# Loading x in 64 KB runs and y through one buffer, in a kernel for the softmax of row-wise dot products

## The chip, the cores and the metric

The kernel runs on one core of a Trainium2 chip. The metric is the device time of one execution in microseconds (us), and the median of several executions is quoted. The profile of an execution has a span, from the first instruction to the last, that is shorter than its time, because the time also holds what lies before and after these.

A load is issued into a queue, and 16 DMA engines work the queue off in packets, each of which the trace records. The load has landed when its semaphore, a counter that others wait on, has been raised. For each load an engine also moves a 4-byte completion packet, which takes 9 ns.

## The reference

```python
B, N, D = 8, 4096, 512            # x and y: [8, 4096, 512], float32
gram = np.matmul(x, y.transpose(0, 2, 1))
diag = np.diagonal(gram, axis1=1, axis2=2)
diag = diag - diag.max(axis=-1, keepdims=True)
exp = np.exp(diag)
return exp / exp.sum(axis=-1, keepdims=True)     # [8, 4096]
```

Only the diagonal is needed: 4096 dot products of length 512 per batch, then a softmax over the 4096. So 134.2 MB are read, each byte is used once, and 0.13 MB are written.

## The kernel before

A batch is laid out with 32 rows on each of 128 partitions, and the 32 rows of a partition are one contiguous run of 64 KB in memory. The kernel takes half a batch at a time, so x and y each come in 4 MB loads made of 128 runs of 32 KB. Three pairs of buffers rotate.

```python
R = N // P          # 32 rows per partition
H = R // 2          # half a batch: 16 rows
io = tile_pool(bufs=3)

def load(b, r0, parts):
    xt = io.tile([P, H, D], f32);  yt = io.tile([P, H, D], f32)
    o = 0
    for n in parts:
        nc.sync.dma_start(out=xt[:, o:o+n, :], in_=xv[b, :, r0+o : r0+o+n, :])
        nc.sync.dma_start(out=yt[:, o:o+n, :], in_=yv[b, :, r0+o : r0+o+n, :])
        o += n
    return xt, yt

def dots(b, r0, xt, yt):                 # the wide form: product in place, then the sum
    nc.vector.tensor_tensor(out=xt, in0=xt, in1=yt, op=mult)
    nc.vector.tensor_reduce(out=diag[:, c:c+H], in_=xt, axis=X, op=add)

# dots_by_row: one scalar_tensor_tensor per row, with accum_out (product and sum at once)
# softmax(b): max on VectorE, all-reduce on GpSimd, -max on VectorE, exp with sum on ScalarE,
#             all-reduce on GpSimd, reciprocal and scaling on VectorE, store from ScalarE's queue
# ... (cut)
for b in range(B):
    for h in range(2):
        n = 2 * b + h
        parts = {2*B-2: [8, 8], 2*B-1: [8, 4, 2, 1, 1]}.get(n, [H])
        xt, yt = load(b, h * H, parts)
        (dots_by_row if n >= 2*B-3 else dots)(b, h * H, xt, yt)
    softmax(b)
```

Of the kernel before, what the change touches and what calls it, by code (L numbers as in the profile page):

```python
# [1 line left out]

# [5 lines left out]


@with_exitstack
def kernel(
    ctx: ExitStack,
    tc: tile.TileContext,
    x: bass.AP,
    y: bass.AP,
    out: bass.AP,
):
    nc = tc.nc
    f32 = mybir.dt.float32  # L20
    B, N, D = x.shape
    P = nc.NUM_PARTITIONS
    R = N // P
    H = R // 2


    xv = x.rearrange("b (p r) d -> b p r d", p=P)
    yv = y.rearrange("b (p r) d -> b p r d", p=P)
    ov = out.rearrange("b (p r) -> b p r", p=P)

    io = ctx.enter_context(tc.tile_pool(name="io", bufs=3))
    persist = ctx.enter_context(tc.tile_pool(name="persist", bufs=1))
    sm = ctx.enter_context(tc.tile_pool(name="sm", bufs=2))

    diag = persist.tile([P, B * R], f32, name="diag")
    res = persist.tile([P, B * R], f32, name="res")

    def load(b, r0, parts):
        xt = io.tile([P, H, D], f32, tag="xt", name="xt")
        yt = io.tile([P, H, D], f32, tag="yt", name="yt")  # L40
        o = 0
        for n in parts:
            nc.sync.dma_start(out=xt[:, o : o + n, :], in_=xv[b, :, r0 + o : r0 + o + n, :])  # L43
            nc.sync.dma_start(out=yt[:, o : o + n, :], in_=yv[b, :, r0 + o : r0 + o + n, :])  # L44
            o += n
        return xt, yt

    def dots(b, r0, xt, yt):
        c = b * R + r0
        nc.vector.tensor_tensor(out=xt, in0=xt, in1=yt, op=mybir.AluOpType.mult)  # L50
        nc.vector.tensor_reduce(  # L51
            out=diag[:, c : c + H], in_=xt, axis=mybir.AxisListType.X, op=mybir.AluOpType.add
        )

    def dots_by_row(b, r0, xt, yt):
        for k in range(H):
            c = b * R + r0 + k
            nc.vector.scalar_tensor_tensor(  # L58
                out=xt[:, k, :],
                in0=xt[:, k, :],  # L60
                scalar=1.0,
                in1=yt[:, k, :],
                op0=mybir.AluOpType.mult,
                op1=mybir.AluOpType.mult,
                accum_out=diag[:, c : c + 1],
            )

    def softmax(b):
        db = diag[:, b * R : (b + 1) * R]
        rb = res[:, b * R : (b + 1) * R]  # L70
        mxp = sm.tile([P, 1], f32, tag="mxp", name="mxp")
        nc.vector.tensor_reduce(out=mxp, in_=db, axis=mybir.AxisListType.X, op=mybir.AluOpType.max)  # L72
        mx = sm.tile([P, 1], f32, tag="mx", name="mx")
        nc.gpsimd.partition_all_reduce(out_ap=mx, in_ap=mxp, channels=P, reduce_op=bass_isa.ReduceOp.max)  # L74
        nmx = sm.tile([P, 1], f32, tag="nmx", name="nmx")
        nc.vector.tensor_single_scalar(out=nmx, in_=mx, scalar=-1.0, op=mybir.AluOpType.mult)  # L76
        sump = sm.tile([P, 1], f32, tag="sump", name="sump")
        nc.scalar.activation(  # L78
            out=rb, in_=db, func=mybir.ActivationFunctionType.Exp,
            bias=nmx, scale=1.0, accum_out=sump,  # L80
        )
        ssum = sm.tile([P, 1], f32, tag="ssum", name="ssum")
        nc.gpsimd.partition_all_reduce(out_ap=ssum, in_ap=sump, channels=P, reduce_op=bass_isa.ReduceOp.add)  # L83
        rc = sm.tile([P, 1], f32, tag="rc", name="rc")
        nc.vector.reciprocal(out=rc, in_=ssum)  # L85
        nc.vector.tensor_single_scalar(out=rb, in_=rb, scalar=rc, op=mybir.AluOpType.mult)  # L86
        nc.scalar.dma_start(out=ov[b], in_=rb)

    for b in range(B):
        for h in range(2):  # L90
            n = 2 * b + h
            parts = {2 * B - 2: [8, 8], 2 * B - 1: [8, 4, 2, 1, 1]}.get(n, [H])
            xt, yt = load(b, h * H, parts)
            (dots_by_row if n >= 2 * B - 3 else dots)(b, h * H, xt, yt)
        softmax(b)


# [1 line left out]
_INS = ['x', 'y']  # L99
_OUTS = [((8, 4096), 'float32')]  # L100


# [23 lines left out]
```

## Time and profile before

| | |
|---|---|
| time | 323.26 us, median of 3 runs (323.23 to 323.59) |
| span of the profile | 321.6 us (an execution of 323.94 us) |
| load queue busy | 97.5% of the 16 DMA engines' span |
| VectorE busy | 261.4 us (81%) |

These lines are from the page of the kernel before: the span, the busy times, the rates in 40 slices of the span, and the table of DMA queues (queue, packets, MB, share of 16 engines' span). q1 carries the loads, q10 the stores.

```profile
span 321.6 us, 345 instructions
DVE 261.4 (81%) x154; ACT 4.6 (1%) x17; POOL 6.1 (2%) x20
...
DMA  8999999999999999999999999999999999999991
GB/s 326 456 395 452 440 408 456 391 458 391 456 412 436 454 395 456 440 408 458 416 432 456 392 458 440 408 456 417 433 449 395 456 437 412 424 424 426 427 407 53
...
q1 hardware_dynamic: 6048, 134.22, 97.5%
q10 hardware_dynamic: 1152, 0.13, 0.3%
```

The load queue is busy from the start to the end. The packets of q1 add up to 313.5 us per engine. VectorE (DVE) has work for 261 us only.

The list of waits (engine, line, what was waited for: us in total, times, longest) shows VectorE waiting for y, and its groups of instructions show what it does. Each group has the line, the operation, the operands and the count, then the busy time in us and the mean of one in ns, then the idle time before them.

```profile
DVE xt L50 <- DMA yt<-in_y_dram: 34.5, 8, 22.6
DVE xt L58 <- DMA yt<-in_y_dram: 9.7, 4, 4.7
```

```profile
L50 DVE TENSOR_TENSOR xt<-xt,yt 128x8192 f32<-128x8192 f32 x13 | 113.0, 8689 | 34.5 <-DMA yt<-in_y_dram 34.5
L51 DVE TENSOR_REDUCE diag<-xt 128x16 f32<-128x8192 f32 x13 | 112.9, 8686 | 0.4
L58 DVE SCALAR_TENSOR_TENSOR xt<-xt,yt 128x512 f32<-128x512 f32 x48 | 30.0, 687 | 9.9 <-DMA yt<-in_y_dram 9.7
```

The chain that ended last, in order of time (start in us, duration, what), contains the wide products and sums:

```profile
42.03 8.70 DVE xt L50
50.74 0.02 issue
50.76 8.70 DVE diag L51
...
79.12 0.33 SPq L43
79.44 0.05 issue
79.50 40.70 DMA yt<-in_y_dram
```

This chain says that a sum on VectorE releases a buffer and that a load is then issued. The load takes 40.7 us from issue to landing, but 4 MB take only 9.7 us at the rate of this trace. For the rest of the time the load stands in the queue behind others.

The packet records give the cost of a run (here a contiguous stretch of memory). A packet of 32 KB takes 1213 ns (median), 16 KB 612, 8 KB 312, 4 KB 161 and 2 KB 86.

### The profile page before, as it was taken

The numbers are of one execution on the slowest core, as the hardware profiler recorded it, in microseconds if no ns is written. First come the engines' busy times: TensorE is split into PE (matmuls) and PEld (weight loads), VectorE is DVE, ScalarE is ACT, GpSimd is POOL, SyncE is SP. The second block draws the span as 40 slices with busy tenths as digits, with TensorE's granted clock in tenths as the row PEclk, the third lists the DMA queues.
The fourth block names the chain that finished last, engine by engine and source line by source line (L and its number), as shares of the span: only waits on it lengthen the run. The fifth ranks groups of instructions, "written<-read, shape, count | busy, mean of one in ns | idle before, by whom it ended". The sixth has DMA issues, their size and how long they took to land.

```text
span 321.6 us, 345 instructions
## 1 busy us (share of the span) xinstructions
DVE 261.4 (81%) x154; ACT 4.6 (1%) x17; POOL 6.1 (2%) x20
## 2 busy tenths in 40 slices
DVE  0019979898998979979799897989979799776494
ACT  1000000000000000000000000000000000000000
POOL 0000000000000000000000000000000000000000
DMA  8999999999999999999999999999999999999991
GB/s 326 456 395 452 440 408 456 391 458 391 456 412 436 454 395 456 440 408 458 416 432 456 392 458 440 408 456 417 433 449 395 456 437 412 424 424 426 427 407 53
DMA packets 7201, 134.36 MB, mean 418 GB/s; under 512 B 1824, under 2 KB 1824, under 8 KB 2592
## 3 DMA queue, kind: packets, MB, share of 16 engines
q1 hardware_dynamic: 6048, 134.22, 97.5%
q10 hardware_dynamic: 1152, 0.13, 0.3%
q14 instruction: 1, 0.01, 0.0%
HBM read 134.22 MB, written 0.13 MB: 418 GB/s over the span
## 4 chain that ended last, share of the span: by engine, by line
DMA 63%; DVE 33%; issue 1%; SPq 1%; POOL 1%; ACT 0%; POOLq 0%; DVEq 0%
DMA yt<-in_y_dram 63%; DVE xt L50 16%; DVE diag L51 16%; SPq L43 1%; POOL mx L74 0%; POOL ssum L83 0%; DVE mxp L72 0%; DVE xt L58 0%; ACT res L78 0%; DVE rc L85 0%; POOLq L121 0%; SPq L44 0%; DVE res L86 0%; DVE nmx L76 0%; DVEq L50 0%
## 5 line engine op out<-in xcount | busy, mean ns | idle before, releaser
L50 DVE TENSOR_TENSOR xt<-xt,yt 128x8192 f32<-128x8192 f32 x13 | 113.0, 8689 | 34.5 <-DMA yt<-in_y_dram 34.5
L51 DVE TENSOR_REDUCE diag<-xt 128x16 f32<-128x8192 f32 x13 | 112.9, 8686 | 0.4
L58 DVE SCALAR_TENSOR_TENSOR xt<-xt,yt 128x512 f32<-128x512 f32 x48 | 30.0, 687 | 9.9 <-DMA yt<-in_y_dram 9.7
L74 POOL PARTITION_ALL_REDUCE mx<-mxp x8 | 2.8, 352 | 306.6 <-DVE mxp L72 306.6
L85 DVE RECIPROCAL rc<-ssum 128x1 f32<-128x1 f32 x8 | 1.3, 164 | 7.7 <-POOL ssum L83 7.7
L78 ACT ACTIVATE res<-diag,nmx 128x32 f32<-128x32 f32 x8 | 2.6, 321 | 312.9 <-DVE nmx L76 312.9
L76 DVE TENSOR_SCALAR nmx<-mx 128x1 f32<-128x1 f32 x8 | 1.2, 154 | 4.3 <-POOL mx L74 4.3
L58 DVE DVE_READ_ACCUMULATOR xt<-xt,yt 128x1 f32 x48 | 3.9, 82 | 0.0
L83 POOL PARTITION_ALL_REDUCE ssum<-sump x8 | 3.1, 385 | 5.8 <-ACT res L78 5.8
L86 DVE TENSOR_SCALAR res<-res,rc 128x32 f32<-128x32 f32 x8 | 1.9, 242 | 0.9
L72 DVE TENSOR_REDUCE mxp<-diag 128x1 f32<-128x32 f32 x8 | 1.5, 186 | 0.3
L78 ACT ACTIVATION_READ_ACCUMULATOR res<-diag,nmx 128x1 f32 x8 | 1.5, 186 | 0.0
L78 ACT ACT_TABLE_LOAD x1 | 1.3, 1283 | 0.7 <-PEq L110 0.7
L110 POOL MEMSET const-float32-0.0<- 128x1 f32 x1 | 0.1, 100 | 0.2 <-issue 0.2
L110 POOL MEMSET const-bfloat16-1.0<- 128x1 bf16 x1 | 0.1, 102 | 0.0
L110 POOL MEMSET const-uint8-127<- 128x1 uint8 x1 | 0.1, 102 | 0.0
L110 POOL MEMSET const-float32-1.0<- 128x1 f32 x1 | 0.1, 99 | 0.0
## 6 DMA issues: line engine op xcount, KB each, us to landing
xt<-in_x_dram SPq DMA_DIRECT2D x14, 4096.0 KB, 31.2
yt<-in_y_dram SPq DMA_DIRECT2D x14, 4096.0 KB, 40.5
xt<-in_x_dram SPq DMA_DIRECT2D x3, 2048.0 KB, 27.1
yt<-in_y_dram SPq DMA_DIRECT2D x3, 2048.0 KB, 31.6
xt<-in_x_dram SPq DMA_DIRECT2D x1, 1024.0 KB, 31.9
yt<-in_y_dram SPq DMA_DIRECT2D x1, 1024.0 KB, 29.5
xt<-in_x_dram SPq DMA_DIRECT2D x1, 512.0 KB, 25.8
yt<-in_y_dram SPq DMA_DIRECT2D x1, 512.0 KB, 22.2
```

Of the source, the lines that this page charges most:

```text
L43: nc.sync.dma_start(out=xt[:, o : o + n, :], in_=xv[b, :, r0 + o : r0 + o + n, :])
L50: nc.vector.tensor_tensor(out=xt, in0=xt, in1=yt, op=mybir.AluOpType.mult)
L51: nc.vector.tensor_reduce(out=diag[:, c : c + H], in_=xt, axis=mybir.AxisListType.X, op=mybir.AluOpType.add)
L58: nc.vector.scalar_tensor_tensor(out=xt[:, k, :], in0=xt[:, k, :], scalar=1.0, in1=yt[:, k, :], op0=mybir.AluOpType.mult, op1=mybir.AluOpT ...
L72: nc.vector.tensor_reduce(out=mxp, in_=db, axis=mybir.AxisListType.X, op=mybir.AluOpType.max)
L74: nc.gpsimd.partition_all_reduce(out_ap=mx, in_ap=mxp, channels=P, reduce_op=bass_isa.ReduceOp.max)
L76: nc.vector.tensor_single_scalar(out=nmx, in_=mx, scalar=-1.0, op=mybir.AluOpType.mult)
L78: nc.scalar.activation(out=rb, in_=db, func=mybir.ActivationFunctionType.Exp, bias=nmx, scale=1.0, accum_out=sump,)
L83: nc.gpsimd.partition_all_reduce(out_ap=ssum, in_ap=sump, channels=P, reduce_op=bass_isa.ReduceOp.add)
L85: nc.vector.reciprocal(out=rc, in_=ssum)
L86: nc.vector.tensor_single_scalar(out=rb, in_=rb, scalar=rc, op=mybir.AluOpType.mult)
L110: nc = _bacc.Bacc("TRN2", target_bir_lowering=False, num_devices=1)
```

## The change

The intent is fewer and longer packets, and a softmax that disturbs VectorE less often. x of a batch is loaded at once, in runs of 64 KB, into one of two 64 KB buffers per partition. y has only one 64 KB buffer, which is filled in halves. Together they take the 192 KB per partition that the six buffers took before. Products are written over x. The softmaxes of batches 0 to 4 and of 5 and 6 are done in two groups with one store each, and the order on each engine is fixed by hand. All of batch 6 is done row by row.

```diff
-    xt = io.tile([P, H, D]);  yt = io.tile([P, H, D])         # three of each
+    xs = [big.tile([P, R, D], f32, name=f"xs{i}") for i in range(2)]
+    ys = big.tile([P, R, D], f32, name="ys")
 ... (cut)
-    for b in range(B):
-        for h in range(2):
-            ... load(b, h * H, parts); dots or dots_by_row
-        softmax(b)
+    for b in range(wide):                       # wide = B - 2
+        load_x(b, 0, R)                         # 8 MB in 64 KB runs
+        for r0 in (0, R // 2):
+            load_y(b, r0, R // 2)               # 4 MB in 32 KB runs
+            dots_wide(b, r0, R // 2)            # products over x
+        if b == wide - 1:
+            group_out("a", 0, wide - 1, first)  # scale and store batches 0 to 4
+        sums_wide(b)                            # one sum for the whole batch
+        if b == wide - 2:
+            first = group_exp("a", 0, wide - 1)
+    b = B - 2
+    load_x(b, 0, R)
+    ... load_y in halves, dot_row for each of the 32 rows
+    b = B - 1
+    r0 = 0
+    for n in (8, 8, 8, 4, 2, 1, 1):
+        load_x(b, r0, n);  load_y(b, r0, n)
+        for r in range(r0, r0 + n):
+            if r == 2:
+                second = group_exp("b", B - 3, 2)
+            if r == 10:
+                group_out("b", B - 3, 2, second)
+            dot_row(b, r)
+        r0 += n
+    last_softmax(b)
```

In the groups, ScalarE does the negation and the scaling, which VectorE did before.

More of the change, by code (lines that the diff above doesn't have):

```diff
@@ L19 @@
     nc = tc.nc
+    ctx.enter_context(tc.manual_schedule())
     f32 = mybir.dt.float32
+    Alu = mybir.AluOpType
+    Act = mybir.ActivationFunctionType
+    X = mybir.AxisListType.X
     B, N, D = x.shape
@@ L23 @@
     R = N // P
-    H = R // 2
+    wide = B - 2
     xv = x.rearrange("b (p r) d -> b p r d", p=P)
     yv = y.rearrange("b (p r) d -> b p r d", p=P)
-    ov = out.rearrange("b (p r) -> b p r", p=P)
-    io = ctx.enter_context(tc.tile_pool(name="io", bufs=3))
-    persist = ctx.enter_context(tc.tile_pool(name="persist", bufs=1))
-    sm = ctx.enter_context(tc.tile_pool(name="sm", bufs=2))
-    diag = persist.tile([P, B * R], f32, name="diag")
-    res = persist.tile([P, B * R], f32, name="res")
@@ L38, in load @@
-    def load(b, r0, parts):
-        xt = io.tile([P, H, D], f32, tag="xt", name="xt")
-        yt = io.tile([P, H, D], f32, tag="yt", name="yt")
-        o = 0
-        for n in parts:
-            nc.sync.dma_start(out=xt[:, o : o + n, :], in_=xv[b, :, r0 + o : r0 + o + n, :])
-            nc.sync.dma_start(out=yt[:, o : o + n, :], in_=yv[b, :, r0 + o : r0 + o + n, :])
-            o += n
-        return xt, yt
-    def dots(b, r0, xt, yt):
-        c = b * R + r0
-        nc.vector.tensor_tensor(out=xt, in0=xt, in1=yt, op=mybir.AluOpType.mult)
-        nc.vector.tensor_reduce(
-            out=diag[:, c : c + H], in_=xt, axis=mybir.AxisListType.X, op=mybir.AluOpType.add
-        )
@@ L55, in dots_by_row @@
-    def dots_by_row(b, r0, xt, yt):
-        for k in range(H):
-            c = b * R + r0 + k
-            nc.vector.scalar_tensor_tensor(
-                out=xt[:, k, :],
-                in0=xt[:, k, :],
-                scalar=1.0,
-                in1=yt[:, k, :],
-                op0=mybir.AluOpType.mult,
-                op1=mybir.AluOpType.mult,
-                accum_out=diag[:, c : c + 1],
-            )
-    def softmax(b):
-        db = diag[:, b * R : (b + 1) * R]
-        rb = res[:, b * R : (b + 1) * R]
-        mxp = sm.tile([P, 1], f32, tag="mxp", name="mxp")
-        nc.vector.tensor_reduce(out=mxp, in_=db, axis=mybir.AxisListType.X, op=mybir.AluOpType.max)
-        mx = sm.tile([P, 1], f32, tag="mx", name="mx")
-        nc.gpsimd.partition_all_reduce(out_ap=mx, in_ap=mxp, channels=P, reduce_op=bass_isa.ReduceOp.max)
-        nmx = sm.tile([P, 1], f32, tag="nmx", name="nmx")
-        nc.vector.tensor_single_scalar(out=nmx, in_=mx, scalar=-1.0, op=mybir.AluOpType.mult)
-        sump = sm.tile([P, 1], f32, tag="sump", name="sump")
-        nc.scalar.activation(
-            out=rb, in_=db, func=mybir.ActivationFunctionType.Exp,
-            bias=nmx, scale=1.0, accum_out=sump,
-        )
-        ssum = sm.tile([P, 1], f32, tag="ssum", name="ssum")
@@ new lines, with column, load_x @@
+    ov = out.rearrange("b (p r) -> p b r", p=P)
+    big = ctx.enter_context(tc.tile_pool(name="big", bufs=1))
+    small = ctx.enter_context(tc.tile_pool(name="small", bufs=1))
+    xs = [big.tile([P, R, D], f32, name=f"xs{i}") for i in range(2)]
+    ys = big.tile([P, R, D], f32, name="ys")
+    diag = small.tile([P, B, R], f32, name="diag")
+    res = small.tile([P, B, R], f32, name="res")
+    def column(name, n):
+        return small.tile([P, n], f32, name=name)
+    def load_x(b, r0, n):
+        nc.sync.dma_start(out=xs[b % 2][:, r0 : r0 + n, :], in_=xv[b, :, r0 : r0 + n, :])
@@ new lines, in load_y, with dots_wide, sums_wide, dot_row @@
+    def load_y(b, r0, n):
+        nc.sync.dma_start(out=ys[:, r0 : r0 + n, :], in_=yv[b, :, r0 : r0 + n, :])
+    def dots_wide(b, r0, n):
+        xt = xs[b % 2][:, r0 : r0 + n, :]
+        nc.vector.tensor_tensor(out=xt, in0=xt, in1=ys[:, r0 : r0 + n, :], op=Alu.mult)
+    def sums_wide(b):
+        nc.vector.tensor_reduce(out=diag[:, b, :], in_=xs[b % 2], axis=X, op=Alu.add)
+    def dot_row(b, r):
+        xt = xs[b % 2]
+        nc.vector.scalar_tensor_tensor(
+            out=xt[:, r, :],
+            in0=xt[:, r, :],
+            scalar=1.0,
+            in1=ys[:, r, :],
+            op0=Alu.mult,
+            op1=Alu.mult,
+            accum_out=diag[:, b, r : r + 1],
+        )
@@ new lines, in group_exp @@
+    def group_exp(name, b0, n):
+        mxp, mx, nmx, sump, ssum = (column(name + s, n) for s in ("mxp", "mx", "nmx", "sump", "ssum"))
+        nc.vector.tensor_reduce(out=mxp, in_=diag[:, b0 : b0 + n, :], axis=X, op=Alu.max)
+        nc.gpsimd.partition_all_reduce(out_ap=mx, in_ap=mxp, channels=P, reduce_op=bass_isa.ReduceOp.max)
+        nc.scalar.mul(nmx, mx, -1.0)
+        for i in range(n):
+            nc.scalar.activation(
+                out=res[:, b0 + i, :], in_=diag[:, b0 + i, :], func=Act.Exp,
+                bias=nmx[:, i : i + 1], scale=1.0, accum_out=sump[:, i : i + 1],
+            )
+        nc.gpsimd.partition_all_reduce(out_ap=ssum, in_ap=sump, channels=P, reduce_op=bass_isa.ReduceOp.add)
+        return ssum
@@ new lines, in group_out, with last_softmax @@
+    def group_out(name, b0, n, ssum):
+        rc = column(name + "rc", n)
+        nc.vector.reciprocal(out=rc, in_=ssum)
+        for i in range(n):
+            rb = res[:, b0 + i, :]
+            nc.scalar.activation(out=rb, in_=rb, func=Act.Copy, scale=rc[:, i : i + 1])
+        nc.scalar.dma_start(out=ov[:, b0 : b0 + n, :], in_=res[:, b0 : b0 + n, :])
+    def last_softmax(b):
+        db, rb = diag[:, b, :], res[:, b, :]
+        mxp, mx, nmx, sump, ssum, rc = (column("l" + s, 1) for s in ("mxp", "mx", "nmx", "sump", "ssum", "rc"))
+        nc.vector.tensor_reduce(out=mxp, in_=db, axis=X, op=Alu.max)
+        nc.gpsimd.partition_all_reduce(out_ap=mx, in_ap=mxp, channels=P, reduce_op=bass_isa.ReduceOp.max)
+        nc.vector.tensor_single_scalar(out=nmx, in_=mx, scalar=-1.0, op=Alu.mult)
+        nc.scalar.activation(out=rb, in_=db, func=Act.Exp, bias=nmx, scale=1.0, accum_out=sump)
@@ L83, in softmax @@
         nc.gpsimd.partition_all_reduce(out_ap=ssum, in_ap=sump, channels=P, reduce_op=bass_isa.ReduceOp.add)
-        rc = sm.tile([P, 1], f32, tag="rc", name="rc")
         nc.vector.reciprocal(out=rc, in_=ssum)
-        nc.vector.tensor_single_scalar(out=rb, in_=rb, scalar=rc, op=mybir.AluOpType.mult)
-        nc.scalar.dma_start(out=ov[b], in_=rb)
-    for b in range(B):
-        for h in range(2):
-            n = 2 * b + h
-            parts = {2 * B - 2: [8, 8], 2 * B - 1: [8, 4, 2, 1, 1]}.get(n, [H])
-            xt, yt = load(b, h * H, parts)
-            (dots_by_row if n >= 2 * B - 3 else dots)(b, h * H, xt, yt)
-        softmax(b)
+        nc.vector.tensor_single_scalar(out=rb, in_=rb, scalar=rc, op=Alu.mult)
@@ new lines, in last_softmax @@
+        nc.scalar.dma_start(out=ov[:, b, :], in_=rb)
+    for b in range(wide):
[10 more added lines that the diff above has]
+    load_x(b, 0, R)
+    for r0 in (0, R // 2):
+        load_y(b, r0, R // 2)
+        for r in range(r0, r0 + R // 2):
+            dot_row(b, r)
@@ L99 @@
+    b = B - 1
+    r0 = 0
+    for n in (8, 8, 8, 4, 2, 1, 1):
+        load_x(b, r0, n)
+        load_y(b, r0, n)
+        for r in range(r0, r0 + n):
[3 more added lines that the diff above has]
+                group_out("b", B - 3, 2, second)
+            dot_row(b, r)
+        r0 += n
+    last_softmax(b)
 _INS = ['x', 'y']
```

## The prediction

> **What bounds the kernel now.** The loads. In the table of DMA queues the load queue is busy for 97.5% of 16 engines' span, and the packet records show its packets without a gap from 1.7 to 315.7 us of the 321.6 us span. VectorE is busy 81% (261.4 us), and in the list of waits it waits 34.5 us for y before the wide products: it is ahead of the loads. The chain of waits gives DVE 33%, but those pieces release buffers for loads that then stand in the queue (y: 40.5 us from issue to landing), so they cost nothing. After the last landing (316.1 us) come 5.5 us: the last row, the softmax and its store.
>
> **How fast a packet is.** A 32 KB packet takes 1213 ns, 16 KB 612, 8 KB 312, 4 KB 161: about 11 ns each plus 27.26 bytes per ns, so 16 engines reach at most 436 GB/s however long the runs. The Trainium skill ("DMA: Bandwidth & Descriptors", Where 436 GB/s comes from) gives 435.2 GB/s as the ceiling of the SBUF ports; this trace agrees. Only the 11 ns are left to win.
>
> **What the change does** (times are estimates from the durations above, 8.69 us for a product and 9.7 us for 4 MB).
> 1. x of seven batches in 64 KB runs: 56 packets fewer per engine, 56 x 11 ns = 0.6 us less; nothing if 64 KB is cut in two. The bytes stay.
> 2. One y buffer: the load of a half waits for the product with the half before it, but is issued about 20 us before its turn. x of batch b+2 waits for the 17.4 us sum of batch b and comes 12 us before its turn. VectorE needs 34.8 us of a batch of 38.8. The queue never runs dry.
> 3. Softmaxes in groups: some 2 us fewer on VectorE per batch grouped, all hidden. The last softmax is unchanged.
> 4. Three stores for eight, the same 128-byte packets, which take turns with load packets (the skill, same page, "Queues, rings and completion order"; here 9 store packets took 9 to 10 us beside 32 KB loads). The group of five has 41 per engine: some 40 us to landing, near 288 us. The group of two is issued near 296 us and lands near 308; the load of x's last row reuses its semaphore and waits for that; its turn is at 313. Tight, but it fits.
> 5. The parts of batch 7's loads are the same.
>
> **On the critical path:** item 1 and about 0.1 us of completion packets.
>
> **Predicted time:** 322.6 us; 321.2 to 324.8 holds it 8 times in 10. Faster by over 2%: 0.02; within 2%: 0.94; slower by over 2%: 0.04.
>
> **What would show each step right or wrong.** (1) 64 KB packets of about 2415 ns, or 32 KB ones. (2) The load queue's share stays at 97 to 98%, no slice but first and last below 390 GB/s; VectorE waits for y in every batch, its first product starts at about 31.5 us instead of 22.6, at no cost. (3) VectorE busy within 5 us of 261. (4) The five-batch store's issue to landing near 40 us. (5) The last y landing near 315.5 us and 5.5 us after it.
>
> **What would make it wrong.** 64 KB runs cut into small packets, or slower per byte; a load whose issue waits for VectorE until the queue is dry; a store that lands late and holds up the last row's load (a gap in the last 10 us); rows that queue on VectorE in the tail.

## The result, and the profile after

The changed kernel takes 322.39 us, the median of 4 runs (322.32 to 322.48). The kernel before takes 323.34 us in the same rounds. The ratio is 0.997, with a 95% interval of 0.9952 to 0.9987. A ratio is the mean time of one kernel's runs over that of the other's in the same rounds, so it is not quite the ratio of the medians.

The same lines of the page after:

```profile
span 320.5 us, 318 instructions
DVE 248.9 (78%) x154; ACT 6.2 (2%) x26; POOL 3.3 (1%) x10
...
DMA  9999999899999999989999999999999999999991
GB/s 393 393 393 458 429 421 523 348 438 491 425 393 429 421 458 401 515 364 421 515 401 393 442 409 458 450 401 450 401 523 393 394 448 407 425 429 427 421 410 59
...
q1 hardware_dynamic: 5040, 134.22, 97.4%
q10 hardware_dynamic: 1072, 0.13, 0.3%
```

The load queue is as full as before, with about a thousand packets fewer. The packet records hold 896 packets of 65,536 bytes with a median of 2420 ns, so a run of 64 KB is one packet. The packets of q1 add up to 312.3 us per engine instead of 313.5. The span is 1.1 us shorter, and so is this sum.

This agreement is better than it should be, because the profiled execution of the kernel before was a slow one. The kernel before has a median span of 321.2 us in each of the three sets below (27 runs), the changed kernel 320.6 us in its four runs here and 320.9 and 320.8 us in sets 1 and 3. So only 0.3 to 0.6 us of the gain lies inside the span. The other 0.5 us lies outside it: the time is 2.3 us longer than the span in the kernel before (2.24 to 2.35) and 1.8 us in the changed kernel (1.75 to 1.82). No packet of a load lies there. What fills this time was not tested.

The waits and groups of VectorE after:

```profile
DVE xs L55 <- DMA ys<-in_y_dram: 53.6, 12, 32.4
DVE xs L62 <- DMA ys<-in_y_dram: 13.6, 5, 4.8
```

```profile
L55 DVE TENSOR_TENSOR xs<-xs,ys 128x8192 f32<-128x8192 f32 x12 | 104.3, 8692 | 53.6 <-DMA ys<-in_y_dram 53.6
L58 DVE TENSOR_REDUCE diag<-xs 128x32 f32<-128x16384 f32 x6 | 103.3, 17220 | 0.2
L62 DVE SCALAR_TENSOR_TENSOR xs<-xs,ys 128x512 f32<-128x512 f32 x64 | 40.0, 688 | 13.8 <-DMA ys<-in_y_dram 13.6
```

VectorE waits longer for y than before, 67.2 us in all instead of 44.2, in a span of nearly the same length. It has 12.5 us less to do, and in the softmaxes it waits 10.5 us less for GpSimd (1.5 us instead of 12.0 in the two lists of waits).

The chain after has the same shape, with one product per batch that releases half of the y buffer:

```profile
79.85 29.96 DMA ys<-in_y_dram
109.81 0.03 issue
109.84 0.02 DVEq L55
109.86 0.04 issue
109.91 8.71 DVE xs L55
118.61 0.02 issue
118.63 29.96 DMA ys<-in_y_dram
```

Of the 29.96 us from the issue of y to its landing, 9.7 are its own transfer. It was issued about 20 us before its turn. The table of DMA issues (what, queue, count, KB where it is known, median us from issue to landing) tells the same of x, and gives the stores. An x of 8 MB takes 19.4 us to transfer (8 packets of 2.42 us per engine), so it comes about 13 us before its turn.

```profile
xs<-in_x_dram SPq DMA_DIRECT2D x7, 32.1
out_dram<-res ACTq DMA_DIRECT2D x1, 80.0 KB, 40.4
out_dram<-res ACTq DMA_DIRECT2D x1, 32.0 KB, 10.5
out_dram<-res ACTq DMA_DIRECT2D x1, 16.0 KB, 1.4
```

### The profile page after: what moved, and what is told of

Same layout as the page of the kernel before. It is cut to its first block, busy times and chain, and to the rows that moved or that the text cites. A ratio compares the mean times of both kernels' runs of the same rounds, so it can differ in the third digit from the quotient of the medians.

```text
span 320.5 us, 318 instructions
## 1 busy us (share of the span) xinstructions
DVE 248.9 (78%) x154; ACT 6.2 (2%) x26; POOL 3.3 (1%) x10
## 3 DMA queue, kind: packets, MB, share of 16 engines
q1 hardware_dynamic: 5040, 134.22, 97.4%
## 4 chain that ended last, share of the span: by engine, by line
DMA 77%; DVE 20%; issue 1%; SPq 0%; POOLq 0%; ACT 0%; POOL 0%; DVEq 0%; ACTq 0%
DMA ys<-in_y_dram 74%; DVE xs L55 16%; DVE xs L62 4%; DMA out_dram<-res 3%; SPq L48 0%; POOLq L162 0%; ACT res L91 0%; POOL lmx L98 0%; DVE res L103 0%; DVE lmxp L97 0%; DVE lrc L102 0%; DVEq L55 0%; DVE brc L88 0%; DVEq L62 0%; DVEq L103 0%
## 5 line engine op out<-in xcount | busy, mean ns | idle before, releaser
L55 DVE TENSOR_TENSOR xs<-xs,ys 128x8192 f32<-128x8192 f32 x12 | 104.3, 8692 | 53.6 <-DMA ys<-in_y_dram 53.6
L58 DVE TENSOR_REDUCE diag<-xs 128x32 f32<-128x16384 f32 x6 | 103.3, 17220 | 0.2
L62 DVE SCALAR_TENSOR_TENSOR xs<-xs,ys 128x512 f32<-128x512 f32 x64 | 40.0, 688 | 13.8 <-DMA ys<-in_y_dram 13.6
L62 DVE DVE_READ_ACCUMULATOR xs<-xs,ys 128x1 f32 x64 | 5.3, 83 | 0.0
L79 ACT ACTIVATE res<-diag,anmx 128x32 f32<-128x32 f32 x5 | 1.5, 309 | 0.0
L91 ACT ACTIVATE res<-res,arc 128x32 f32<-128x32 f32 x5 | 1.2, 309 | 19.0 <-DVE arc L88 19.0
L76 POOL PARTITION_ALL_REDUCE bmx<-bmxp x1 | 0.7, 736 | 60.5 <-DVE bmxp L75 60.5
L79 ACT ACTIVATION_READ_ACCUMULATOR res<-diag,anmx 128x1 f32 x5 | 0.9, 187 | 0.0
L83 POOL PARTITION_ALL_REDUCE bssum<-bsump x1 | 0.8, 797 | 1.1 <-ACT res L79 1.1
```

Source lines behind the costliest of these rows:

```text
L55: nc.vector.tensor_tensor(out=xt, in0=xt, in1=ys[:, r0 : r0 + n, :], op=Alu.mult)
L58: nc.vector.tensor_reduce(out=diag[:, b, :], in_=xs[b % 2], axis=X, op=Alu.add)
L62: nc.vector.scalar_tensor_tensor(out=xt[:, r, :], in0=xt[:, r, :], scalar=1.0, in1=ys[:, r, :], op0=Alu.mult, op1=Alu.mult, accum_out=diag ...
L76: nc.gpsimd.partition_all_reduce(out_ap=mx, in_ap=mxp, channels=P, reduce_op=bass_isa.ReduceOp.max)
L79: nc.scalar.activation(out=res[:, b0 + i, :], in_=diag[:, b0 + i, :], func=Act.Exp, bias=nmx[:, i : i + 1], scale=1.0, accum_out=sump[:, i ...
L83: nc.gpsimd.partition_all_reduce(out_ap=ssum, in_ap=sump, channels=P, reduce_op=bass_isa.ReduceOp.add)
```

## The experiments

The theory is this. The loads are the bound, every engine but the DMA has time to spare, and the only thing the change can win is the fixed cost of the packets that it saves. There are three rivals for the 1 us. The first is that it comes from fewer stores and grouped softmaxes. The second is that it is an accident. The third is that VectorE, through the buffers it frees, has a share in the bound after all. Twelve runs of ten kernels were made in three sets, and every run of a set was on the same chip. "Above the changed kernel" is the difference of the medians of the same set where that set holds the changed kernel.

### Set 1: is it the packets?

The changed kernel again, unedited.

> The changed kernel once more, on the chip of the other runs of this set: 322.4 us, ratio to before 0.997. If the 1 us it won was an accident of one chip or one set of runs, the ratio is 1.000.

It took 322.65 us (322.50 to 322.76), ratio 0.9972 (0.9959 to 0.9984). The gain repeats on another set of executions, so it is no accident.

x in 32 KB runs:

```diff
 def load_x(b, r0, n):
-    nc.sync.dma_start(out=xs[b % 2][:, r0 : r0 + n, :], in_=xv[b, :, r0 : r0 + n, :])
+    step = min(n, R // 2)
+    for o in range(r0, r0 + n, step):
+        nc.sync.dma_start(out=xs[b % 2][:, o : o + step, :], in_=xv[b, :, o : o + step, :])
```

> The changed kernel with x of a batch loaded by two loads in 32 KB runs, all else kept. Theory (the gain is the packets): 56 pairs of 1213 ns instead of packets of 2420 ns per engine give 0.34 us, seven more loads with their completion packets 0.06 us: 0.4 us above the changed kernel, so 322.8 us. Rival (the gain comes from fewer stores, grouped softmaxes or the fixed order): no difference from the changed kernel, within 0.1 us.

It took 323.39 us (323.33 to 323.61), which is 0.74 us above the changed kernel. Its ratio to before is 0.9996. With the 32 KB runs nearly all of the gain is gone, although the single y buffer, the groups and the fixed order are still there. The rival that expected no difference is out. The size is more than the 0.4 us expected from the median packet durations. The spans say more. Of the 0.74 us, 0.5 lie inside the span (medians 321.4 and 320.9 us) and 0.23 outside (the time is 2.0 us longer than the span, instead of 1.8). Against the kernel before, which has as many load packets, this variant is 0.2 us longer inside the span and 0.3 us shorter outside. So the rest of the change is not without effect: its two effects nearly cancel.

x in 8 KB runs:

```diff
 def load_x(b, r0, n):
+    if n < R: ...                                   # batch 7 as it was
-    nc.sync.dma_start(out=xs[b % 2][:, r0 : r0 + n, :], in_=xv[b, :, r0 : r0 + n, :])
+    xt = xs[b % 2].rearrange("p (c a k) d -> p a c (k d)", a=2, k=4)
+    xd = xv[b].rearrange("p (c a k) d -> p a c (k d)", a=2, k=4)
+    for a in range(2):                              # even blocks of 4 rows, then odd ones
+        nc.sync.dma_start(out=xt[:, a], in_=xd[:, a])
```

> The changed kernel with x of a batch loaded by two loads in 8 KB runs (even blocks of four rows, then odd ones). Theory (a fixed cost of each packet, and nothing else, tells run lengths apart): 8 packets of 309 to 312 ns for each of 2420: +52 to +76 ns, times 56: 2.9 to 4.3 us above the changed kernel, so 325.3 to 326.7 us. Rival (run length as such is of no account while the queue is full; the 0.3% came from elsewhere): within 0.5 us of the two loads in 32 KB runs.

It took 326.54 us (326.42 to 326.64), which is 3.89 us above the changed kernel, within the expected 2.9 to 4.3. The bytes, the number of loads and the work of every engine are those of the 32 KB variant, so the runs alone (their length, and the order of blocks that comes with it) cost 3.15 us here.

A softmax and a store for each batch:

```diff
 for b in range(wide):
     load_x(b, 0, R)
     for r0 in (0, R // 2):
         load_y(b, r0, R // 2)
         dots_wide(b, r0, R // 2)
-    if b == wide - 1:
-        group_out("a", 0, wide - 1, first)
     sums_wide(b)
-    if b == wide - 2:
-        first = group_exp("a", 0, wide - 1)
+    last_softmax(b)
 ... (likewise batch 6, in place of the second group)
```

> The changed kernel with a softmax and a store for each batch, as before, x still in 64 KB runs. Theory: the store packets are the same, five more completions per engine are 0.05 us, and VectorE's wait for each softmax (about 2 us a batch) fits into its idle 3 to 4 us: within 0.15 us of the changed kernel. Rival (the eight stores were what cost the kernel before its 1 us): 0.4 to 0.9 us above the changed kernel.

It took 322.85 us (322.81 to 322.93), which is 0.20 us above the changed kernel and just outside the 0.15 that the theory allowed. The two ranges do not overlap, so grouping is worth something, but the rival's 0.4 to 0.9 us is not there. In the traces the packets of q1 take 312.3 us per engine here and 312.4 in the changed kernel, so the 0.2 us is not in the loads' packets. Nor does it show in the spans, whose medians are 320.9 us for both. Most of it lies outside the span: the time is 1.88 to 1.95 us longer than the span here, and 1.75 to 1.80 us in the changed kernel. What fills it was not tested.

### Set 2: the same law at its extreme, and the spare time of VectorE

x in 2 KB runs, the edit of the 8 KB variant with k=1.

> The changed kernel with x of a batch loaded by two loads in 2 KB runs (even rows, then odd ones). Theory (a fixed cost of each packet): 32 packets of 86 ns for each of 2420: +332 ns, times 56: 18.6 us above the changed kernel, near 341 us; 15 to 20 us above if packets so short overlap each other a little, as the 8 KB ones did. Rival (run length as such is of no account): no more above it than the 8 KB runs, 3.9 us.

It took 339.02 us (338.86 to 339.14), ratio 1.0479. Set 2 does not hold the changed kernel. Against its time in set 1 this is 16.37 us above, inside the 15 to 20 us expected (the kernel before took 323.50 us in set 1 and 323.49 in set 2). The load queue's share rose to 99.6% with the same bytes:

```profile
q1 hardware_dynamic: 32928, 134.22, 99.6%
```

VectorE on an eighth of the columns. The result is wrong (relative error 1.37), but every load, wait and store is kept:

```diff
-nc.vector.tensor_tensor(out=xt, in0=xt, in1=ys[:, r0 : r0 + n, :], op=Alu.mult)
+nc.vector.tensor_tensor(out=xt[:, :, 0:64], in0=xt[:, :, 0:64], in1=ys[:, r0 : r0 + n, 0:64], op=Alu.mult)
 ... (likewise the sum and the form by row)
```

> The changed kernel with VectorE's products and sums over 64 of each row's 512 columns: a wrong result on purpose, with every load, wait and store kept. Theory (the loads are the bound, VectorE costs nothing until the last row): VectorE's busy time falls from 249 to some 45 us, the time only by the shorter last row, 0.5 to 0.7 us: 321.8 to 322.2 us, ratio 0.995 to 0.996. Rival (buffers freed by VectorE hold loads up somewhere): 2 us or more below the changed kernel.

It took 322.01 us (321.92 to 322.18), ratio 0.9956, about 0.6 us below the changed kernel. From the page:

```profile
span 320.1 us, 318 instructions
DVE 39.8 (12%) x154; ACT 6.2 (2%) x26; POOL 2.6 (1%) x10
...
GB/s 393 393 393 454 426 430 516 344 450 467 450 393 409 442 459 393 516 356 438 491 426 393 414 438 459 393 454 418 438 499 418 390 415 441 409 431 432 418 411 76
```

Taking away 209 us of VectorE's 249 wins about 0.6 us. Most of it is the one row that follows the last landing, which takes 0.23 us in place of 0.69. The loads now stand in the queue for longer: a half of y takes 37.5 us from issue to landing (30.0 in the changed kernel), an x of 8 MB 54.5 us (32.1). This is the plainest evidence that VectorE is not in the bound. The slices of 344 and 356 GB/s stand here too, with VectorE nearly idle, so in the changed kernel they are not a queue waiting for VectorE.

The sums of the six wide batches done twice:

```diff
 def sums_wide(b):
+    nc.vector.tensor_reduce(out=diag[:, b, R - 32 : R], in_=xs[b % 2][:, R - 32 : R, :], axis=X, op=Alu.add)
     nc.vector.tensor_reduce(out=diag[:, b, :], in_=xs[b % 2], axis=X, op=Alu.add)
```

> The changed kernel with the sum over 32 rows done twice in the six wide batches: 17.2 us more of VectorE per batch, far over its idle 3.9 us. Theory (buffers come free too late once VectorE needs more than the 38.8 us that a batch's loads take): 52 us a batch on VectorE, so its sixth sum ends near 345 us, the loads of batch 7 start there, 39 us of loads follow, and about 7 us: near 392 us, 386 to 398. The load queue then shows gaps. Rival (spare VectorE time is not what hides the single y buffer): under 340 us.

It took 394.65 us (394.51 to 395.16), inside the range and 2.7 us above its middle. The page shows what a queue that runs dry looks like:

```profile
DVE 350.9 (89%) x160; ACT 6.2 (2%) x26; POOL 17.9 (5%) x10
...
GB/s 354 494 380 427 481 427 374 427 160 427 427 427 320 0 427 427 427 427 0 320 427 417 434 110 214 427 400 444 224 107 427 377 436 370 0 320 429 439 408 119
...
q1 hardware_dynamic: 5040, 134.22, 80.6%
```

There are slices of 0 GB/s, and the queue's share falls to 80.6%. So the time that VectorE has to spare does hide the single y buffer, and the arrangement fails once that time is used up.

The second store moved later:

```diff
-            if r == 10:
+            if r == 24:
                 group_out("b", B - 3, 2, second)
```

> The changed kernel with the scaling and store of batches 5 and 6 moved from before row 10 to before row 24 of batch 7, about 13 us later. Theory (the load of the last row of x waits for this store because both use one semaphore): the store is issued near 309.8 us, lands near 313 to 314, the last two loads are issued then instead of 307.6, and the last landing moves from 315 to 316.5 or 317: 1.5 to 2.5 us above the changed kernel. Rival (a small store at the end costs nothing): within 0.3 us of it.

It took 322.63 us (322.43 to 322.96), the same as the changed kernel in set 1. The expectation was missed because the experiment did not do what it was meant to do. The semaphores are handed out in an order that depends on where the store stands. With the store in its new place all loads have been issued before it (the last at 307.65 us, the store at 310.91), so none waits for it. In its stead an earlier load of y in batch 7 waits 10.3 us for the store of batches 0 to 4 ("SPq L51 <- DMA out_dram<-res: 10.3, 1, 10.3"), also at no cost. What the run does show is the reverse. In the changed kernel the load of the last row of x waited 7.4 us for this store ("SPq L48 <- DMA out_dram<-res: 7.4, 1, 7.4" in the list of the DMA queue's waits), and a kernel without that wait is no faster. So the wait costs nothing as it stands. What a store that really lands too late would cost was not measured.

### Set 3: the size of a packet's cost, and a little more VectorE

The changed kernel a third time.

> The changed kernel a third time, as the measure for the other runs of this set: ratio to before 0.997.

It took 322.57 us (322.56 to 323.10), ratio 0.9974.

x in 32 KB runs again, unedited from set 1.

> x in 32 KB runs again. The 8 KB and 2 KB runs gave 9.9 and 9.4 ns for each packet more (3.89 us over 392 packets, 16.37 us over 1736). By that, 56 packets more are 0.53 us, with seven more completions 0.6 us above the changed kernel; the first time it was 0.74. Rival (the 0.74 holds something besides packets): 0.7 to 0.9 us again.

It took 323.37 us (323.13 to 323.54), which is 0.80 us above by the medians. The ratios, 0.9994 and 0.9974, give 0.65 us.

x in 16 KB runs, the edit of the 8 KB variant with k=8.

> The changed kernel with x of a batch loaded by two loads in 16 KB runs. Theory (9.4 to 9.9 ns for each packet more): 168 packets more, 1.6 to 1.7 us, and 0.06 us for completions: 1.7 us above the changed kernel. Rival (a cost of 0.74 us for two loads in place of one, whatever the runs): 1.9 us or more.

It took 324.48 us (324.43 to 324.57), which is 1.91 us above by the medians and 1.75 by the ratios (1.0028 and 0.9974). Between the two expectations this run alone does not decide.

All run lengths together, with the packets more than in the changed kernel counted per DMA engine:

| x in runs of | packets more | us above the changed kernel | ns per packet more |
|---|---|---|---|
| 64 KB | 0 | 0 | |
| 32 KB | 56 | 0.74 and 0.80 | 13 and 14 |
| 16 KB | 168 | 1.91 | 11.4 |
| 8 KB | 392 | 3.89 | 9.9 |
| 2 KB | 1736 | 16.37 | 9.4 |

From 32 KB to 2 KB, where the number of loads is the same, the slope is (16.37 - 0.77) us / 1680 packets = 9.3 ns per packet. At 32 KB this slope explains 56 x 9.3 ns = 0.52 us of the 0.77. About 0.25 us is left over, so the 0.77 does hold something besides packets, as the rival of the second 32 KB run said. It looks like a cost of two loads in place of one, because the slope with this remainder also gives the 8 KB run (3.64 + 0.25 = 3.89 us) and nearly the 16 KB run (1.56 + 0.25 = 1.81). The spans and the packet records show that it is not one cost:

- In the 32 KB runs 0.23 us lies outside the span (2.0 us instead of 1.8, in both sets).
- In the 16, 8 and 2 KB runs the time outside the span is 1.8 us, as in the changed kernel, but the first packet of q1 starts 0.4 us later (2.14 to 2.16 us instead of 1.72).
- From the start of the first packet of q1 to the end of the last, the traces have 313.05 us for the changed kernel in sets 1 and 3, then 313.46 and 313.56 (32 KB), 314.43 (16 KB), 316.59 (8 KB) and 328.96 (2 KB). That is 7 to 9 ns for each packet more at every length, with an estimated 0.06 us for seven more completion packets included.

So the packets alone account for 0.4 to 0.5 us between 32 KB and 64 KB runs. Why the time before the first packet and outside the span differs stays open.

A little more work for VectorE, the edit of the doubled sums with 4 rows in place of 32:

> The changed kernel with the sum over the last four rows done twice in the six wide batches: 2.15 us more of VectorE per batch, within its idle 3.9 us. Theory (VectorE's spare time hides it): within 0.1 us of the changed kernel. Rival (every VectorE microsecond delays a load, as the chain of waits might be read): 6 x 2.15 = 12.9 us above it.

It took 322.61 us (322.50 to 322.93), 0.04 us above the changed kernel. The page and the two lists of waits (VectorE's, and the DMA queue's own):

```profile
DVE 262.6 (82%) x160; ACT 6.2 (2%) x26; POOL 9.9 (3%) x10
```

```profile
DVE xs L55 <- DMA ys<-in_y_dram: 42.4, 12, 32.3
```

```profile
SPq L48 <- DVE diag L59: 95.8, 5, 19.2
```

VectorE works 13.7 us more and waits 11.2 us less for y before the wide products. The issuing of x waits longer for the sums (the changed kernel's line is "SPq L48 <- DVE diag L58: 84.2, 5, 16.8"), and the time is the same. In these runs a wait of the issuing queue for VectorE costs nothing while earlier loads still stand in the queue.

## Why the prediction was right

The predicted 322.6 us met 322.39, and "within 2%" met 0.3%. That the bound stays and the time hardly moves was foreseen for the right reason. That the number came so close is in part luck. The sum was 0.7 us less than 323.26 (item 1 and completion packets), and 0.3 to 0.6 us of gain inside the span answer to it. The other 0.5 us, outside the span, stands in no item of the prediction.

- **The bound.** Right, and shown. An eighth of VectorE's elements wins about 0.6 us, 13.7 us more of its work costs nothing, while more packets for the same bytes move the time nearly in proportion to their number.
- **Item 1, 0.6 us from 56 packets of 11 ns.** The mechanism is right. One 64 KB packet appeared (2420 ns, expected 2415), and going back to 32 KB gives back 0.74 to 0.80 of 0.85 to 0.96 us. The cost of a packet is 9.3 ns by the runs, where the fit of durations gave 11. The term was therefore a little large: 56 packets are worth 0.4 to 0.5 us, and most of the rest of the 0.74 to 0.80 us lies outside the span (0.23) and between the last packet and the last instruction (0.1).
- **Item 2, the single y buffer.** Right. The loads of y were issued about 20 us before their turn and those of x about 13 us before (predicted 20 and 12). The first product started at 32.4 us (predicted 31.5), and this late start did not show in the time. One check was badly chosen: "no slice but first and last below 390 GB/s". Slices of 348 and 364 GB/s are there, but each has a neighbour of over 510, and the nearly idle VectorE shows the same pattern. The likely reason, not tested, is that with packets of 64 KB that last 2.4 us the bytes of an 8 us slice depend on which packets are counted in it. The queue's share of 97.4% is the reading to trust.
- **Item 3, the grouped softmaxes.** "All hidden" was nearly right: undoing the groups costs 0.20 us. The check "VectorE busy within 5 us of 261" failed, for the profile has 248.9. The step that failed is "some 2 us fewer on VectorE per batch grouped" as the whole account. Most of these 2 us were waits, for the four small VectorE operations of a softmax are busy for 0.75 us together, and so the check allowed 5 us. It left out that the first half of batch 6 moves from the wide form (8.69 + 8.69 us) to rows (16 rows at 0.613 us each, from one start to the next, 9.8 us), 7.6 us less. The rest is the small operations of the softmax and the sum of a whole batch (17.22 us instead of twice 8.69). As VectorE has time to spare, the miss did not touch the time.
- **Item 4, the stores.** Right. The store of five batches took 40.4 us to land (predicted 40). The second store was issued at 297.1 us and landed near 307.6 (predicted 296 and 308), and the load that waited for it was issued at 307.6 us, and the run with the store in another place shows that this wait cost nothing.
- **Item 5, the tail.** Right. The last landing was at 315.0 us and 5.5 us came after it, as before.

## What to carry to other kernels

When a load queue is full from end to end, as here, its bytes and its packets set the time. Count the packets that a change saves, multiply by the fixed cost of one (7 to 9 ns here, where a 32 KB packet as a whole takes 1.2 us), and expect no more than that from the loads. Compare spans as well as times, and look at whether the profiled execution was a typical one: here half of a gain of 1 us lay outside the span, and a slow profile hid that. A single buffer was as good as several because the engine that frees it was done before the load's turn in the queue. Compare the time from issue to landing with the transfer's own duration, and the difference is the margin. A chain of waits that runs through another engine is no proof that this engine counts, so take its work away, or add some, and look at the time.

## What the Trainium skill lacked or had wrong

- "DMA: Bandwidth & Descriptors", Where 436 GB/s comes from: its ceiling of 435.2 GB/s agrees (32 KB packets of 1213 ns on 16 engines are 432 GB/s). Its note beside the figure says that for transfers between HBM and SBUF the HBM side, about 358 GB/s, binds. With one core at work the kernels before and after show a mean of 418 and 419 GB/s over the whole span, near the 425 GB/s that the page itself measured for one core. The page says under its measurements that 358 is a core's share when both cores of a pair stream, so the note misleads only when it is read alone.
- The same page, Why small descriptors are slow: it names a fixed overhead per packet and advises about descriptors of 256 bytes and less. Elsewhere the page gives about 10.5 ns per packet, but for a 4 KB transfer of 64 packets. It lacks the cost for long runs in a full queue: 9.3 ns per packet, that is 16.37 us of 339.02 with 44% of the data in 2 KB runs, and 0.4 to 0.5 us between 32 KB and 64 KB runs. It also does not say outright that a run of 65,536 bytes goes as one packet (896 packets, 2420 ns).
- The same page, Queues, rings and completion order: it says that an engine drains a whole packet of typically 9 to 17 descriptors from one queue before it turns to the next. Here 40 store descriptors of 128 bytes per engine went out beside 37.6 load packets per engine in 36.5 us, so about one for one. This fits a store of 80 KB taking 40.4 us to land beside long loads, and 8.0 us beside loads in 2 KB runs.
